# First norm's gain and offset moved behind the gather and into later experts, and a tenth weight tile, in a transformer block with 32 experts

## The chip, the core and the metric

The kernel runs on one core of a Trainium2 chip. A core has TensorE (PE, matrix multiplies, with its weight loads shown apart as PEld), VectorE (DVE), ScalarE (ACT), GpSimd (POOL) and the issuing engine SyncE (SP). Sixteen transfer engines (DMA) move data between the chip's memory (HBM), the on-chip SBUF and the accumulators of TensorE (PSUM). The metric is the time of one execution on the device, in microseconds (us).

## The reference

One layer of an encoder over 256 tokens of 1024 numbers, in float32. The first half is attention in two branches with gates; it ends in an output projection. What the change touches is what follows:

```python
x = layer_norm(ALPHA * x + mix, ln1_g, ln1_b)         # mix: the attention half
x = layer_norm(ALPHA * x + moe(x), ln2_g, ln2_b)

def layer_norm(x, g, b):
    return (x - mean(x)) * rsqrt(var(x) + 1e-5) * g + b     # g, b: one number a column

def moe(x):                                            # 32 experts, each token goes to 4
    logits = x @ w_router + b_router                   # 1024 x 32
    top_v, top_i = top_k(logits, 4)
    gates = softmax(top_v)
    # for each token and each of its four experts e:
    h = x @ w_mlp1[e] + b_mlp1[e]                      # 1024 x 2048
    glu, lin = min(h[::2], 7), clip(h[1::2], -7, 7)
    a = glu * sigmoid(1.702 * glu) * (lin + 1)
    y += gate * (a @ w_mlp2[e] + b_mlp2[e])            # 1024 x 1024
```

An expert has 12 MB of weights, all 32 together 403 MB of the 439 MB that the kernel reads.

## The kernel before

**Weights in tiles.** Weights come in tiles of 2 MB (128 partitions of 16 KB), two chunks each. An expert has four tiles for its first layer (`m1`, chunks 0 to 7) and two for its second (`m2`, chunks 0 to 3). `seq` sets the order: `m1` of expert 0, then for each further expert e its `m1` and after it `m2` of expert e - 1, at last `m2` of expert 31. `queue` lists the tiles; `feed` (L88) takes the next and issues its load on SP, `refill` (L120) calls it after a tile's second chunk, into the place just used. SP issues in order: a load waits there until its place is free. Nine places hold weights when the experts begin: five of `ring`, two of `ring2` (freed by the split weights of the first half), `ring4` and `ring3` (in the place `qq`). Other buffers are tags of the pool `big`: "nh", "xh", "xl", "v" and "an" are used one after the other by tiles of different stages.

**From the projection to the experts.** From L588 on the order is written by hand (`manual_schedule`): every engine carries out its part in program order. `residual` forms ALPHA * x + mix and its statistics, `normal` the normed tokens, `affine` (L613) times gain plus offset, three of four halves on GpSimd. `turn` transposes the normed tokens, `logits` multiplies by the router's weights (gain and offset are folded into those, L499) with experts on the partitions, `logits_rows` transposes back. `choose` finds the four experts of each token, `count` and `place` its slot in each expert (64 slots, CAP), `pick` builds a matrix P of ones that says which token sits in which slot, and `gather_mm` (L704) multiplies the tokens by P: `XS`, the transposed tokens of four experts, in eight column blocks k.

**In the experts.** `m1` multiplies `XS` by the weights into two PSUM banks, copies the result to `hs`; `activate` transposes it, adds the bias and applies the gate; `m2` multiplies by the second layer's weights into one bank ("tp"), `gate_o` scales it by the gate and splits it in two float32r parts `oh` and `ol`; `combine` (L835) adds them, by token, to Y in PSUM. `onehot` prepares the combine's matrix. What else is done beside is hung by `at` behind a chunk: the gather of the next four experts (L892 to L894), the biases of the second layers at expert 8, the loading and spreading of the second norm's gain and offset (`load_ln2` behind chunk 1 of expert 28's first layer, `spread_ln2` (L874) behind chunks 3 and 4 of experts 29's and 30's first layers). Y starts as ALPHA times the first norm's result: `y_start` (L844), four multiplies by a scaled unit matrix `alid`, three in the router stretch and one behind chunk 1 of expert 1.

**The end.** After the last combine the statistics of Y are completed, and the second norm is applied and stored.

The functions, with the profile's line numbers:

Of the kernel before, what the change touches and what calls it, by code (L numbers as in the profile page):

```python
# [17 lines left out]
D = 1024  # L18
NE = 32
# [12 lines left out]
def block_kernel(ctx: ExitStack, tc: tile.TileContext, x, xT, w_in, cols_in, b_v, lam_v,  # L32
# [55 lines left out]
    def feed(where=ring_tile):  # L88
# [22 lines left out]
        kind, e, c = seq[2 * u - N1]  # L111
# [48 lines left out]
    br = keep.tile([NE, 2], F32, name="br")  # L160
# [385 lines left out]
    for i in range(N1):  # L546
# [11 lines left out]
        if i == N1 - 1:  # L558
            for j in range(SPL):
# [9 lines left out]
        if i == 23:  # L569
            feed(lambda: big.tile([128, 4096], F32, name="ring3", tag="qq"))  # L570
# [19 lines left out]
    x1 = big.tile([128, 2, D], F32, name="x1", tag="nh")  # L590
# [37 lines left out]
    def logits(t):  # L628
        pl = pp.tile([128, 512], F32, name="tp", bufs=1)
# [3 lines left out]
        lt_ = keep.tile([NE, 128], F32, name="lgT", bufs=1)  # L633
        act(lt_, pl[:NE, 0:128], AF.Identity, bias=br[:, 1:2])
        lgs[t] = lt_

    def logits_rows(t):
        p = pp.tile([128, 512], F32, name="pv", bufs=1)
        nc.tensor.transpose(p[:, 0:NE], lgs[t], ident[:NE, :NE])
        lgs[t] = p  # L640

    def choose(t):
        pl = lgs[t][:, 0:NE]
        m8 = keep.tile([128, 8], F32, name="m8", bufs=2)
        nc.vector.max(out=m8, in_=pl)
        nm = keep.tile([128, 2], F32, name="nm", bufs=2)
# [486 lines left out]
```

## Time and profile before

| | us |
|---|---|
| median of 3 runs (lowest, highest) | 1158.22 (1156.41, 1159.78) |
| the profiled execution | 1158.14 |
| its span, first to last instruction | 1156.4 |
| TensorE busy in the span | 1060.6 (92%) |
| VectorE, ScalarE, GpSimd busy | 368.7, 221.6, 29.1 |
| transfers: 440.83 MB, mean | 381 GB/s |

The page gives busy time by engine, strips of 40 slices, the chain of work that ended last, and the costliest groups of instructions. A busy TensorE is one with a multiply under way, which includes slow ones. "DMA share" is the mean busy share of the 16 transfer engines and can pass 1 a little, since packets overlap. In the timeline a row merges neighbouring instructions of one form; in square brackets stands how long the engine had been idle before it, and what released it. A multiply in float32 is carried out in two passes and counts as two instructions.

### The profile page before, as it was taken

How to read it: one execution, taken by the hardware profiler on the slowest of the kernel's cores; microseconds unless marked ns; L12 is line 12 of the kernel's file. 1: busy time of each engine (PE TensorE's matmuls, PEld its weight loads, DVE VectorE, ACT ScalarE, POOL GpSimd, SP SyncE). 2: the span in 40 equal slices, each digit the busy share in tenths (PEclk: the TensorE clock that was granted, in tenths of full speed). 3: DMA queues.
4: the chain of work that ended last, by engine and by line, in shares of the span. 5: the costliest groups of instructions: out<-in, count | busy, mean ns of one | idle time of the engine just before them, and what ended most of it. 6: DMA issues, size and time to landing. Idle time of an engine off the chain costs nothing.

```text
span 1156.4 us, 12728 instructions
## 1 busy us (share of the span) xinstructions
PE 1060.6 (92%) x5318; PEld 500.7 (43%) x5318; DVE 368.7 (32%) x772; ACT 221.6 (19%) x423; POOL 29.1 (3%) x34
## 2 busy tenths in 40 slices
PE   9999999899999999899899989888999899989984
PEld 8888898533433433333333333332333333322221
DVE  6967757332222222222222122222222221222213
ACT  5475843221111111010001000100010000001111
POOL 0001100200000000000000000000000000000001
PEclk9999999999999999999999999999999999999997
DMA  9953468599999999999999999999999999999992
GB/s 339 382 173 110 164 255 333 216 392 425 426 427 426 426 404 426 426 428 429 426 427 426 427 427 428 427 426 427 426 429 425 427 426 426 427 427 427 427 423 110
DMA packets 48318, 440.83 MB, mean 381 GB/s; under 512 B 5376, under 2 KB 8576, under 8 KB 23424
## 3 DMA queue, kind: packets, MB, share of 16 engines
q1 hardware_dynamic: 47696, 438.91, 91.5%
q8 instruction: 44, 0.72, 0.3%
q0 software_dynamic: 272, 0.53, 0.1%
q10 hardware_dynamic: 288, 0.52, 0.1%
q14 instruction: 18, 0.15, 0.0%
HBM read 438.90 MB, written 1.05 MB: 380 GB/s over the span
## 4 chain that ended last, share of the span: by engine, by line
DMA 57%; PE 29%; issue 6%; DVE 4%; ACT 3%; SPq 0%; POOLq 0%; POOL 0%; ACTq 0%
DMA ring<-in_w_dram 55%; PE sc L773 12%; PE tp L818 5%; PE pj L256 3%; PE pj L440 2%; DMA ring<-in_w_in_dram 2%; PE tp L708 1%; PE pv L708 1%; DVE sp L46 1%; PE pj L271 1%; DMA b1r<-in_b_dram 1%; DVE tm L46 1%; ACT sp L43 1%; PE sc L792 1%; PE pj L841 1%
## 5 line engine op out<-in xcount | busy, mean ns | idle before, releaser
L773 PE MATMUL sc<-ring,XS 128*64 128x512 f32 x2048 | 473.0, 599 | 49.4 <-DMA ring<-in_w_dram 48.7
L773 PEld LDWEIGHTS sc<-ring,XS 128*64 128x64 f32 x2048 | 138.4, 136 | 327.5 <-issue 268.3
L818 PE MATMUL tp<-ring,work 128*64 128x512 f32 x1024 | 235.3, 599 | 20.3 <-DMA ring<-in_w_dram 18.6
L818 PEld LDWEIGHTS tp<-ring,work 128*64 128x64 f32 x1024 | 68.5, 136 | 160.8 <-issue 115.9
L781 DVE COPY hs<-sc 128x512 f32<-128x512 f32 x32 | 22.1, 692 | 320.8 <-PE sc L773 320.8
L256 PE MATMUL pj<-XH,sp 128*128 128x256 f32 x512 | 96.6, 288 | 3.9 <-DVE sp L46 3.6
L256 PEld LDWEIGHTS pj<-XH,sp 128*128 128x128 f32 x512 | 80.6, 192 | 8.3 <-DVE sp L46 4.7
L737 DVE TENSOR_SCALAR GT<-pv,slotp 128x256 fp32r<-128x256 f32 x32 | 15.5, 484 | 197.9 <-PE pv L735 197.9
L46 DVE TENSOR_TENSOR sp<-ring,sp 128x1024 fp32r<-128x1024 f32 (+1 forms) x58 | 68.1, 1188 | 27.2 <-ACT sp L43 27.0
L256 PE MATMUL pj<-XL,sp 128*128 128x256 f32 x256 | 73.2, 286 | 0.0
L43 ACT ACTIVATE sp<-ring 128x1024 fp32r<-128x1024 f32 (+1 forms) x58 | 58.0, 1023 | 67.1 <-PE pj L256 31.0
L46 DVE TENSOR_TENSOR work<-sc,bT 128x512 f32<-128x512 f32 x62 | 42.6, 688 | 74.1 <-PE sc L792 74.1
L43 ACT ACTIVATE as<-work 128x256 f32<-128x256 f32 x64 | 26.7, 417 | 165.0 <-DVE work L799 165.0
L831 DVE SCALAR_TENSOR_TENSOR ol<-tp,GS,oh 128x512 fp32r<-128x512 f32 x32 | 24.0, 751 | 93.8 <-ACT oh L43 93.8
L43 ACT ACTIVATE XS<-pv 128x256 f32<-128x256 f32 x32 | 12.3, 383 | 210.1 <-PE pv L708 210.1
L256 PEld LDWEIGHTS pj<-XL,sp 128*128 128x128 f32 x256 | 49.2, 192 | 0.6 <-issue 0.6
L43 ACT ACTIVATE XS<-tp 128x256 f32<-128x256 f32 x32 | 12.3, 383 | 193.1 <-PE tp L708 193.1
L43 ACT ACTIVATE oh<-tp,GS 128x512 fp32r<-128x512 f32 x32 | 22.0, 687 | 111.4 <-PE tp L818 111.4
L792 PEld LDWEIGHTS sc<-ident,hs 128*128 128x128 f32 x248 | 32.1, 209 | 25.1 <-issue 25.1
L43 ACT ACTIVATE hs<-sc 128x512 f32<-128x512 f32 x32 | 19.1, 597 | 112.9 <-PE sc L773 109.1
L792 PE MATMUL sc<-ident,hs 128*128 128x128 f32 x248 | 38.0, 296 | 0.0
L708 PE MATMUL pv<-P,x 128*128 128x256 f32 x128 | 35.5, 401 | 0.0
(200 smaller groups left out, 742.3 us busy)
## 6 DMA issues: line engine op xcount, KB each, us to landing
ring<-in_w_dram SPq DMA_DIRECT2D x190, 2048.0 KB, 39.1
ring<-in_w_in_dram SPq DMA_DIRECT2D x17, 1024.0 KB, 13.6
ring<-in_w_out_dram SPq DMA_DIRECT2D x4, 1024.0 KB, 6.7
ring<-in_w_dram SPq DMA_DIRECT2D x4, 1024.0 KB, 33.1
ring<-in_w_in_dram SPq DMA_DIRECT2D x4, 512.0 KB, 7.8
nb<-in_rpbx_dram SPq DMA_DIRECT2D x8, 256.0 KB, 3.8
ring<-in_w_da_dram SPq DMA_DIRECT2D x2, 1024.0 KB, 6.1
ring<-in_w_na_dram SPq DMA_DIRECT2D x2, 1024.0 KB, 8.4
```

The source lines that it names most:

```text
L43: return nc.scalar.activation(o, i, f, **kw)
L46: return nc.vector.tensor_tensor(out=o, in0=a, in1=b, op=op)
L256: nc.tensor.matmul(pj[g][:, c], lhsT=a(k, cc), rhs=b[:, kk], start=(kk == 0 and j == 0 and c % 2 == 0), stop=(kk == 7 and j == 2), skip_gr ...
L271: nc.tensor.matmul(pj[g][:, h], lhsT=a[:, kk, hh], rhs=b(k), start=(kk == 0 and j == 0), stop=(kk == 7 and j == 2), skip_group_check=True)
L440: nc.tensor.matmul(y[:, c], lhsT=a(k, cc), rhs=b[:, k], start=(k == 0 and j == 0 and c % 2 == 0), stop=(k == 3 and j == 2), skip_group_che ...
L708: nc.tensor.matmul(px, lhsT=v, rhs=P[g][:, t], start=(t == 0), stop=(t == 1))
L737: nc.vector.tensor_scalar(GT[e], p[:, 256:512], slotp[:, 0:1], None, op0=ALU.is_equal)
L773: nc.tensor.matmul(HP[h][j * CAP:(j + 1) * CAP], lhsT=XS[e // 4][:, c, e % 4], rhs=w[:, h, j], start=(c == 0), stop=(c == 7), skip_group_c ...
L781: nc.vector.tensor_copy(HS[e][:, 1], HP[1])
L792: nc.tensor.transpose(p[:, s, k], v[:, s, k], ident)
L818: nc.tensor.matmul(OP[e][j * CAP:(j + 1) * CAP], lhsT=AS[e][:, c, k], rhs=ring[i][:, n:n + 512], start=(c + k == 0), stop=(c == 3 and k == ...
L831: nc.vector.scalar_tensor_tensor(out=ol, in0=OP[e], scalar=GS[e], in1=oh.bitcast(F32), op0=ALU.mult, op1=ALU.subtract)
```

## The change

1. The first norm's gain and offset are no longer applied to all tokens. `gather` gathers the normed tokens of two experts (columns of 128 instead of 256 a multiply), for two column blocks a call, and ScalarE applies gain and offset as scale and bias of the copy to `XS` (`gbx`, loaded by two GpSimd loads).
2. `residual` and `normal` work in place; the tile `x1` ("nh") goes. `XS` is one tile of two halves in "xh", so "xl" is free too. `hs` and `work` share one tile.
3. "nh" and "xl" hold the two halves of a tenth weight tile (`ring5`), loaded as 1 MB each by `feed_half`: the first behind chunk 23 of the first half, the second behind its last.
4. Y starts with the first combine. ALPHA times the first norm's result is added in experts 3 to 6, a quarter each: `x1_load` fetches gain and offset of both halves into the tile of `oh` (GpSimd, behind chunk 1), `x1_part` spreads one row over the partitions by a multiply and VectorE multiplies or adds it (behind chunks 3 and 4), `y_x1` adds the quarter to Y (behind chunk 6).
5. `logits` has the tokens on the partitions at once, with the bias as a ninth multiply of one row; the ScalarE bias and `logits_rows` go. Copies that only the gates need are taken later (`keep_logits`). The first layers' biases are loaded to "v" and transposed in two halves.
6. The second norm's gain and offset and the output use the first place that is not `ring` and that falls free when no weights are left; they are spread behind the chunks of expert 30's second layer.

```diff
+    def feed_half(s):
+        if s == 0:
+            half[0] = queue.pop(0) if queue else None
...
+        t = ring[2 * u + s] = big.tile([128, 2048], F32, name="ring5", tag=("nh", "xl")[s])
+        if kind == "m1":
+            nc.sync.dma_start(t, m1c(e, c // 2)[:, s])
+        else:
+            nc.sync.dma_start(t.rearrange("p (k c) -> p k c", k=2), m2c(e, c // 2)[:, 2 * s:2 * s + 2])
     def refill(i):
-        if i % 2:
-            feed(home[i // 2])
+        where = home[i // 2]
+        if where == "half":
+            feed_half(i % 2)
+        elif i % 2:
+            if not queue and where is not ring_tile and not lnt:
+                load_ln2(where())
+            else:
+                feed(where)
...
-    def affine(t, h, eng=nc.vector):
-        v = x1[:, t, cut(h)]
-        eng.tensor_tensor(out=v, in0=xn[:, t, cut(h)], in1=late["g"][:, cut(h)], op=ALU.mult)
-        eng.tensor_tensor(out=v, in0=v, in1=late["b"][:, cut(h)], op=ALU.add)
...
+        pl = lgs[t] = pp.tile([128, 512], F32, name=("tp", "pv")[t], bufs=1)
         for k in range(8):
-            nc.tensor.matmul(pl[:NE, 0:128], lhsT=wr[:, k], rhs=x1T[:, k, t * 128:(t + 1) * 128],
-                             start=(k == 0), stop=(k == 7))
+            nc.tensor.matmul(pl[:, 0:NE], lhsT=x1T[:, k, t * 128:(t + 1) * 128], rhs=wr[:, k], start=(k == 0), stop=False)
+        nc.tensor.matmul(pl[:, 0:NE], lhsT=ones[0:1], rhs=br[:, 1], start=False, stop=True)
...
+    def gather(g, k0):
+        px = pp.tile([128, 2, 2, CAP], F32, name="pv" if k0 % 4 else "tp", bufs=1)
+        for u in range(2):
+            k = k0 + u
+            for t in range(2):
+                v = xn[:, t].rearrange("q (c p r) -> q c r p", p=128, r=2)[:, k // 2, k % 2]
+                nc.tensor.matmul(px[:, u], lhsT=v, rhs=P[g][:, t], start=(t == 0), stop=(t == 1))
+        for u in range(2):
+            k = k0 + u
+            act(XS[g][:, k], px[:, u], AF.Identity, scale=gbx[:, 0, k:k + 1], bias=gbx[:, 1, k:k + 1])
...
+    def x1_load():
+        gb = p2b.tile([4, 512], F32, name="gb", tag="oh", bufs=1)
+        for j, src in enumerate((ln1_g, ln1_b)):
+            nc.gpsimd.dma_start(gb[2 * j:2 * j + 2], src.rearrange("(h n) -> h n", h=2))
+        x1p[:] = [gb, p2b.tile([128, 512], F32, name="x1p", tag="ol", bufs=1)]
+    def x1_part(t, h, j):
+        p = pp.tile([128, 512], F32, name="pv", bufs=1)
+        gb, v = x1p
+        nc.tensor.matmul(p, lhsT=ident[0:4, 2 * j + h:2 * j + h + 1].to_broadcast([4, 128]), rhs=gb, start=True, stop=True)
+        tt(v, v if j else xn[:, t, cut(h)], p, ALU.add if j else ALU.mult)
+    def y_x1(t, h):
+        nc.tensor.matmul(Y[t][:, h], lhsT=lstrict, rhs=x1p[1], start=False, stop=False, skip_group_check=True)
...
+            for k in ((0, 2), (4, 6))[e % 2] if e > 1 else ((0,), (2, 4, 6))[e]:
+                at(("m1", e, 5 if e else 7), gather, g, k)
...
+    for e in range(4):
+        t, h = divmod(e, 2)
+        at(("m1", e + 3, 1), x1_load)
+        at(("m1", e + 3, 3), x1_part, t, h, 0)
+        at(("m1", e + 3, 4), x1_part, t, h, 1)
+        at(("m1", e + 3, 6), y_x1, t, h)
...
-    at(("m1", NE - 4, 1), load_ln2)
     for j in range(2):
         for h in range(2):
-            at(("m1", NE - 3 + j, 3 + h), spread_ln2, j, h)
+            at(("m2", NE - 2, 2 * j + h), spread_ln2, j, h)
...
     turn(0)
+    logits(0)
     normal(1)
-    logits(0)
-    affine(1, 0)
-    affine(1, 1, nc.gpsimd)
-    y_start(0, 1)
+    choose(0)
     turn(1)
-    logits_rows(0)
-    choose(0)
-    y_start(0, 0)
     logits(1)
...
+    gather(0, 0)
+    bias_turn(1)
     m1(N1, *seq[0][1:])
-    for k in range(3, 5):
-        gather_mm(0, k)
+    gather(0, 2)
     m1(N1 + 1, *seq[1][1:])
```

How the instructions stand on TensorE from the second logits to the first expert multiplies, before (`x_2037` is the tokens' tile after `affine`, `ring_1577` the first weight tile, L773 `m1`, L846 `y_start`, L756 the transposes of the first layers' biases):

```order
L631 MATMUL tp<-x1T,wr 32x128 x8
L664 MATMUL sc<-maskM,lstrict 128x32
L639 MATMUL pv<-ident,lgT 128x32
L756 MATMUL tp<-ident,b1r 128x64 x8
L663 MATMUL sc<-maskM,ones 128x32
L664 MATMUL sc<-maskM,lstrict 128x32
L846 MATMUL pj<-x_2037,alid 128x512
L708 MATMUL tp<-P,x_2037 128x256 x2
L708 MATMUL pv<-P,x_2037 128x256 x2
L708 MATMUL tp<-P,x_2037 128x256 x2
L773 MATMUL sc<-ring_1577,XS 64x512 x4
```

and now (`xres` is the tokens' tile, L651 and L652 `logits`, L781 the biases, L731 `gather`, L796 `m1`):

```order
L651 MATMUL pv<-wr,x1T 128x32 x8
L652 MATMUL pv<-br,ones 128x32
L680 MATMUL sc<-maskM,lstrict 128x32
L679 MATMUL sc<-maskM,ones 128x32
L680 MATMUL sc<-maskM,lstrict 128x32
L781 MATMUL sc<-ident,b1r 128x64 x4
L731 MATMUL tp<-P,xres 128x128 x4
L781 MATMUL sc<-ident,b1r 128x64 x4
L796 MATMUL sc<-ring_1578,XS 64x512 x4
```

The transposes of the logits and three multiplies into Y are gone, the bias transposes stand in two halves, the second behind the first gather, and one gather of four multiplies stands ahead of the first expert multiplies where three gathers stood.

TensorE in expert 3's first layer, before (L841 `combine`, L735 `onehot`, L708 the gather, L818 `m2`):

```order
L773 MATMUL sc<-ring_2375,XS 64x512 x8
L841 MATMUL pj<-oh,GT 128x512 x4
L841 MATMUL pj<-ol,GT 128x512 x4
L773 MATMUL sc<-ring_2412,XS 64x512 x4
L735 MATMUL pv<-rows,stack 128x512
L773 MATMUL sc<-ring_2412,XS 64x512 x4
L773 MATMUL sc<-ring_2422,XS 64x512 x8
L708 MATMUL tp<-P,x_2037 128x256 x2
L708 MATMUL pv<-P,x_2037 128x256 x2
L773 MATMUL sc<-ring,XS 64x512 x8
L818 MATMUL tp<-ring,work 64x512 x4
```

and now (L864 is `combine`, its second half stands in the first row, L760 `onehot`, L880 `x1_part`, L885 `y_x1`):

```order
L864 MATMUL pj<-ol,GT 128x512 x4
L796 MATMUL sc<-ring,XS 64x512 x4
L760 MATMUL pv<-rows,stack 128x512
L796 MATMUL sc<-ring,XS 64x512 x4
L880 MATMUL pv<-gb,ident 128x512
L796 MATMUL sc<-ring_2415,XS 64x512 x4
L880 MATMUL pv<-gb,ident 128x512
L796 MATMUL sc<-ring_2415,XS 64x512 x4
L731 MATMUL tp<-P,xres 128x128 x4
L731 MATMUL pv<-P,xres 128x128 x4
L796 MATMUL sc<-ring_2425,XS 64x512 x4
L885 MATMUL pj<-x1p,lstrict 128x512
```

Two multiplies by `gb` and one into Y have come in between the chunks; the gather's two calls stay where they were.

TensorE at the end, from the second layer of expert 30 on, before (L818 `m2`, L792 the transposes of expert 31's activation, L841 `combine`):

```order
L818 MATMUL tp<-ring_5746,work 64x512 x4
L792 MATMUL sc<-ident,hs 128x128 x8
L818 MATMUL tp<-ring_5746,work 64x512 x4
L818 MATMUL tp<-ring_5762,work 64x512 x8
L818 MATMUL tp<-ring,work 64x512 x8
L841 MATMUL pj<-oh,GT 128x512 x4
L841 MATMUL pj<-ol,GT 128x512 x4
L818 MATMUL tp<-ring,work 64x512 x8
```

and now (L841 is `m2`, L815 the transposes, L915 `spread_ln2`, L864 `combine`; `ring_6172` is the tile of gain and offset):

```order
L841 MATMUL tp<-ring_6041,hsas 64x512 x4
L815 MATMUL sc<-ident,hsas 128x128 x8
L915 MATMUL pv<-ring_6172,ones 128x512
L841 MATMUL tp<-ring_6041,hsas 64x512 x4
L915 MATMUL pv<-ring_6172,ones 128x512
L841 MATMUL tp<-ring_6066,hsas 64x512 x4
L915 MATMUL pv<-ring_6172,ones 128x512
L841 MATMUL tp<-ring_6066,hsas 64x512 x4
L915 MATMUL pv<-ring_6172,ones 128x512
L841 MATMUL tp<-ring_6076,hsas 64x512 x8
L864 MATMUL pj<-oh,GT 128x512 x4
L864 MATMUL pj<-ol,GT 128x512 x4
```

The four spreads stand now between and behind the chunks of expert 30's second layer. ScalarE's row there, before (`as` is the activation's sigmoid, `warm` the preloading of a table, `oh` empties the second layer's bank):

```order
L43 ACTIVATE hs<-sc 128x512
L43 ACTIVATE as<-work 128x256 x2
L43 ACT_TABLE_LOAD
L43 ACTIVATE warm<-as,eps 1x1
L43 ACTIVATE oh<-tp,GS 128x512 x2
```

and now:

```order
L43 ACTIVATE hsas<-sc 128x512
L43 ACTIVATE as<-gl 128x256 x2
L43 ACT_TABLE_LOAD
L43 ACTIVATE warm<-as,eps 1x1
L43 ACTIVATE ring_6172<-pv 128x512 x3
L43 ACTIVATE oh<-tp,GS 128x512
L43 ACTIVATE ring_6172<-pv 128x512
```

The copies of the spreads stand behind the activation and the table load, three of them ahead of the emptying of expert 30's bank.

## Rows read from the trace of the kernel before

**Rows 1.** The page's strip of GB/s, 40 equal slices of the span

```profile
GB/s 339 382 173 110 164 255 333 216 392 425 426 427 426 426 404 426 426 428 429 426 427 426 427 427 428 427 426 427 426 429 425 427 426 426 427 427 427 427 423 110
```

**Rows 2.** Windows: length, busy time (and count) by engine, granted clock, DMA share, GB/s

```profile
215.00:226.00 11.00, 11.00 (x41) 6.56 (x40) 0.00 (x0) 1.92 (x5) 0.00 (x0) 0.85 0.01 6
236.00:470.00 234.00, 233.66 (x1086) 90.03 (x1084) 57.97 (x141) 27.39 (x57) 2.04 (x4) 1.00 1.01 424
470.00:1121.00 651.00, 583.31 (x2644) 212.36 (x2640) 138.56 (x335) 63.14 (x129) 0.98 (x2) 1.00 1.01 427
```

**Rows 3.** Chain of waits, experts 0 to 6: start us, us, what

```profile
219.44 1.87 PE sc L773 x8
272.33 1.12 PE pj L841 x8
275.75 5.30 PE sc L773 x24
281.05 1.07 PE pv L708 x4
282.12 0.86 PE tp L708 x4
309.69 3.58 PE sc L773 x16
402.40 1.14 PE pj L841 x8
```

**Rows 4.** Timeline of the issue queue SP behind the gap: start us, us, instruction

```profile
225.14 0.33 SPq L118 DMA_DIRECT2D ring<-in_w_dram  x1
232.63 0.33 SPq L113 DMA_DIRECT2D ring<-in_w_dram  x1
```

**Rows 5.** Timeline of the router stretch: start us, us, engine line instruction, idle before

```profile
198.07 1.00 DVE L610 TENSOR_SCALAR xres<-x,bnmv 128x512 f32<-128x512 f32 x2
203.51 1.95 DVE L610 TENSOR_SCALAR xres<-x,bnmv 128x512 f32<-128x512 f32 x2
206.20 1.04 PE L625 MATMUL sc<-ident,xres 128*128 128x128 f32 x8
209.37 1.94 PE L631 MATMUL tp<-x1T,wr 128*32 128x128 f32 x16
212.09 0.20 DVE L645 MAX8 m<-pv 128x8 f32<-128x32 f32 x1 [1.46 <-PE pv L639]
215.14 1.91 PE L708 MATMUL tp<-P,x 128*128 128x256 f32 x4
```

**Rows 6.** DMA issues by tile: queue, count, KB each, us from issue to landing

```profile
wr<-in_w_router_dram SPq DMA_DIRECT2D x1, 128.0 KB, 7.8
work<-in_b_dram POOLq DMA_DIRECT2D x4, 64.0 KB, 7.8
ln<-in_ln_g_dram POOLq DMA_DIRECT2D x1, 4.0 KB, 6.4
ln<-in_ln_b_dram POOLq DMA_DIRECT2D x1, 4.0 KB, 7.2
```

**Rows 7.** Timeline of ln2's spread and of the last two experts

```profile
1051.89 1.12 PE L877 MATMUL pv<-ln,ones 1*128 1x512 f32 x2
1052.94 1.94 PE L773 MATMUL sc<-ring,XS 128*64 128x512 f32 x8
1053.05 0.60 ACT L43 ACTIVATE ln<-pv 128x512 f32<-128x512 f32 x1 [10.78 <-PE pv L877]
1121.36 1.94 PE L818 MATMUL tp<-ring,work 128*64 128x512 f32 x8 [1.34 <-DMA ring<-in_w_dram]
1127.93 0.29 ACT L43 ACTIVATE warm<-as,eps 1x1 f32<-1x1 f32 x1
1131.41 3.65 PE L818 MATMUL tp<-ring,work 128*64 128x512 f32 x16 [1.57 <-DVE ol L831]
```

**Rows 8.** Instructions of line 708: duration ns minimum, median, maximum

```profile
L708 PEld LDWEIGHTS tp<-P,x x128: 192/196/337, 214.6 to 997.5; 128*128 128x128 f32 x128
```

More of the change, by code (lines that the diff above doesn't have):

```diff
@@ L159, in block_kernel @@
     wr = keep.tile([128, 8, NE], F32, name="wr")
-    br = keep.tile([NE, 2], F32, name="br")
+    br = keep.tile([1, 2, NE], F32, name="br")
+    gbx = keep.tile([128, 2, 8], F32, name="gbx")
     make_identity(nc, ident)
@@ L502, in router_fold @@
         for k in range(8):
-            nc.tensor.matmul(p[:NE, 0:1], lhsT=wr[:, k], rhs=b1col[:, k:k + 1], start=(k == 0), stop=(k == 7))
-        tt(br[:, 1:2], br[:, 0:1], p[:NE, 0:1], ALU.add)
+            nc.tensor.matmul(p[0:1, 0:NE], lhsT=b1col[:, k:k + 1], rhs=wr[:, k], start=(k == 0), stop=(k == 7))
+        tt(br[:, 1], br[:, 0], p[0:1, 0:NE], ALU.add)
         tt(wr, wr, g1col.rearrange("p (k o) -> p k o", o=1).to_broadcast([128, 8, NE]), ALU.mult)
@@ L598, in residual @@
     def residual(t, h):
-        v = x1[:, t, cut(h)]
-        nc.vector.scalar_tensor_tensor(out=v, in0=xn[:, t, cut(h)], scalar=ALPHA, in1=OUT[t, h],
-                                       op0=ALU.mult, op1=ALU.add)
+        v = xn[:, t, cut(h)]
+        nc.vector.scalar_tensor_tensor(out=v, in0=v, scalar=ALPHA, in1=OUT[t, h], op0=ALU.mult, op1=ALU.add)
         nc.vector.bn_stats(out=st[t][:, h, :], in_=v)
@@ L835, in combine @@
     def combine(e):
-        for w in OHL[e]:
+        for n, w in enumerate(OHL[e]):
             for t in range(2):
@@ L945, in block_kernel @@
     count(1)
-    y_start(1, 0)
+    bias_turn(0)
     place(1)
     pick(0, slice(1, 2))
-    for k in range(3):
-        gather_mm(0, k)
-    work.append(big.tile([128, 4, 512], F32, name="work", tag="an"))
+    keep_logits(0)
+    keep_logits(1)
+    gather(0, 0)
+    bias_turn(1)
     m1(N1, *seq[0][1:])
-    for k in range(3, 5):
-        gather_mm(0, k)
+    gather(0, 2)
     m1(N1 + 1, *seq[1][1:])
-    for k in range(5, 7):
-        gather_mm(0, k)
+    gather(0, 4)
     m1(N1 + 2, *seq[2][1:])
-    gather_mm(0, 7)
+    gather(0, 6)
     for j, (kind, e, c) in enumerate(seq):
@@ L1047, in block_kernel @@
         row_stats(0)
-    fin = big.tile([128, 2, D], F32, name="fin", tag="qq")
+    lnt, fin = lnt
     row_stats(1)
@@ L1061, in block_kernel @@
         v, y, m = fin[:, t, cut(h)], Y[t][:, h], mv[t]
-        g, b = [lnt[0][:, j, cut(h)] for j in range(2)]
+        g, b = [lnt[:, j, cut(h)] for j in range(2)]
         if (t, h) == (1, 1):
```

141 lines of the change are left out of this document (64 added, 77 removed).

## The prediction

> **What bounds the kernel now.** I read the page's strip of GB/s first [rows 1]: the eighth slice (202 to 231 us) shows 216 between 333 and 392, and from the tenth on nearly all show some 426. The windows say what that is [rows 2]. From 215 to 226 us the transfers stand still (share 0.01), and from 236 to 1121 they never stop (1.01). The nine 2 MB tiles in SBUF are full, and no new one can start before TensorE has used one up: the first issue after the gap stands at 225.14, the second at 232.63 [rows 4], each the refill behind the second chunk of a tile. So nearly all that follows is fixed by when the queue restarts and by how many tiles are then left. The chain of waits bears this out from the other side: it runs through TensorE for the first eight experts, afterwards through the transfers.
>
> TensorE has little to spare at first. From the combine at 272.33 to that at 402.40 lie five experts [rows 3], 26.0 us each. The queue needs 6 x 2.097 MB / 424 GB/s = 29.7 us for the same six tiles [rows 2]. So freed tiles pile up by 3.7 us an expert, and the queue has always one to fill. The third stage is the end: the second multiply of expert 30 starts at 1121.36 behind a transfer, but that of expert 31 waits at 1131.41 for VectorE [rows 7]. From 1121 on TensorE's own order sets the end.
>
> The sum is made against the profiled execution's own 1158.14 us (span 1156.4 and 1.7 around it), 0.08 below the median of the runs.
>
> **The router stretch, earlier restart.** Before, normal(1)'s two halves take 1.95 us at 203.51, beside GpSimd's gains and offsets; normal(0)'s took 1.00 at 198.07, without them. logits(1) starts at 209.37, because TensorE has first to wait for scaled tokens for y_start [rows 5]. Without these, the second half's transposes can start at 204.8 behind logits(0), and logits(1) at 206.1: 3.3 us earlier. It is then 9 multiplies of 32 columns instead of 8 of 128 (1.94 us, row at 209.37). Between the nearest rows I take 2.2. Its end, 208.3, leads straight to VectorE's MAX8; before, a bias on ScalarE and a transpose lay between (209.37 + 1.94 = 211.31 to 212.09). So MAX8 is 3.75 us earlier. The bias transposes, which waited for b1, fall out of this path, since b1 now lands in a tile that is free long before; one half of them is back behind the gather. A y_start in front of the gather goes too, and P's comparison is half as wide: the first gather starts at 210.75 (before 215.14). Before, three gathers led to the expert multiplies of which the row at 219.44 is the first [rows 3]; now one gather and four transposes: 212.5 us at full clock. The granted clock was 0.85 in the mean of 215 to 226 [rows 2], so part of it was at the lower level of 1.2 GHz, after a stretch of short multiplies with gaps. A dip as long would give 214.3. I take 213.4. One gather and two chunks later (5.75 us before, 4.85 now) the first tile is free at 218.2, 6.9 us earlier; the next at 225.2, **7.4 us earlier**.
>
> **The tenth tile.** All ten are loaded before 218, since half one of it fits where the queue idles and half two follows the output projection. When the queue restarts, one tile less is left: 2.097 MB / 427 GB/s = **4.9 us**. Its halves go in 8 KB runs instead of 16 KB. A run's fixed part, an estimate: w_in's runs of 2 KB filled the second slice at 382 GB/s, the 16 KB runs move 427 [rows 1, 2], which per transfer engine (a sixteenth) is 86 and 614 ns a run, so 12 ns a run beside its bytes. Twice the runs in 18 tiles cost 18 x 4.9 x 12/614 = **1.8 us**, between nothing and twice that. If the queue then never starves, the gain is 7.4 + 4.9 - 1.8 = 10.5 us.
>
> **What experts 3 to 6 add.** Each gets three f32 multiplies of 512 columns (two by the broadcast gain and offset, one into Y). Such a one, spread_ln2's, let the next multiply begin 1.05 us later (1051.89 to 1052.94, its busy time 1.12) [rows 7], and a switch of weights costs the next chunk 0.1 to 0.15 (1.87 against 5.30/3) [rows 3]: 3.6 us in all. Of the four y_start removed one stood in expert 1: 1.3 us with its switch. The gather of 128 columns costs more per column: 8 transposes of 128 x 128 took 1.04 us, 0.13 each [rows 5], so a call of 8 parts 1.05 for 0.86 before, and two calls an expert 2.3 for 1.93 [rows 3]: 0.4 more.
>
> And there is a new wait. x1_load's two GpSimd loads overwrite the tile that combine's first half reads. I put their issues at 0.85 and 1.35 us after combine starts: two thirds of its 1.12, and half a us for each issue. TensorE reaches x1_part 5.2 us after that start (combine 1.12, chunk 1.87, the one-hot up to 275.75, a chunk of 5.30/3) [rows 3]. The nearest rows are the two 4 KB loads of the last norm, 6.4 and 7.2 us from issue to landing in a busy queue [rows 6]: the second lands 7.75 to 8.55 after the start. TensorE stands 2.55 to 3.35; I take 2.7, as a queue that has just run dry is less deep. Behind x1_part stand all expert multiplies and thus the next release.
>
> So an expert takes 26.0 + 0.4 + 3.6 + 2.7 = 32.7 us against 29.7: 3.0 us short. What is in hand? From the second release to the last of expert 3's first layer, TensorE took 309.69 + 3.58 - 232.63 = 80.6 us [rows 3, 4]; now 80.6 - 1.3 + 0.2 + 1.4 - 0.5 + 0.4 (y_start; gathers of experts 0 to 3: 1, 3, 2, 2 calls for 1, 2, 3, 2 before) + 3.6 + 2.7 = 87.1. In that time the queue fills 18 tiles, 89.0 us. In hand: 1.9. Experts 4 to 6 lose 3 x 3.0 - 1.9 = **7.1 us**. Of the 10.5, 3.4 remain.
>
> The Trainium skill (DMA: Bandwidth & Descriptors, "Anatomy of one DMA") puts a GpSimd load at about 2.0 us and its bytes. By that gain and offset would be there before TensorE asks, and nothing of the 7.1 us would be lost. The loads of 6.4 and 7.2 us speak against it here; it is a rival below.
>
> **The tail.** spread_ln2 moves from experts 29 and 30, where TensorE waits for transfers, to behind the four chunks of expert 30's second layer. One spread takes 1.05 as above, its copy 0.60 [rows 7]. The first, behind the transposes, ends at 1125.5, but its copy stands on ScalarE behind the activations and the table preload, until 1128.2 [rows 7]. They share one PSUM bank, so the second spread, ready at 1127.3, waits till 1128.85. Third and fourth chunk end at 1131.7 and 1134.6, the third spread between. ScalarE and VectorE empty the bank as before (1.57 us, which hides the fourth): expert 31 starts at 1136.1 instead of 1131.41: **4.7 us later**. Lower bound 0, if the transfers end last after all; upper, 4 x 1.6.
>
> **Small things.** The two gbx loads are 1024 runs of 8 bytes at the start, when the queue is full; wr is as many runs of 128 bytes and landed in 7.8 us beside others [rows 6]. Between nothing and 1.5 us, I take 0.5. The additional ScalarE copies of XS are hidden: TensorE needs them an expert later, and ScalarE is free between.
>
> **Sum:** -10.5 + 7.1 + 4.7 + 0.5 = +1.8: **1159.9 us**.
>
> **Rivals.** *The gain stays* (1152.8): no stall, so 30.0 an expert against 29.7, covered by what is in hand; -10.5 + 5.2. It needs the second load within 3.9 us of its issue; every load on that queue in rows 6 took longer, but none was so small beside an almost empty queue. Half of the stall gone gives 1154.5.
> *Late loads* (1164.9; the slower side): the loads behave like the four of b2, 7.8 us [rows 6], and TensorE stands 3.95 us. 1.25 more an expert in three experts, and nearly as much in the first, is 5 us. Each us of stall costs 4 us, so it is slower than can be told from no change once the second load takes over 7.0 us. For it: the rows of b2 and of the norm's second load, 7.2, lie there. Against: only two rows of 2 KB travel. *Weights exposed* belongs to the same side: a 128 x 128 weight load of the gather took 0.196 us [rows 8]; if no part of it were hidden, a call would take 1.57, 1.0 us more an expert and 4 us up to expert 3: 1166.9. The Trainium skill (TensorE: Matmul & The Clock Gate, "LDWEIGHTS") says that the load costs by its own columns, however few are moved; halving the moved columns doubles the loads per result. The 0.13 us of the transposes says that most is hidden.
> *The tail's spreads cost nothing* (1155.2): the last transfers would have to end later than TensorE's order; the wait on VectorE at 1131.41 is against it.
>
> **Chances.** The measurement tells about 0.3% (3.5 us) from no change. Forecast, within some 4 us of its sum: 0.40. The gain stays: 0.28. Late loads or exposed weights: 0.27. Free tail: 0.05, which stays within 3.5 us of before. The upper end of the forecast's own range, 0.03, is beyond 3.5 us. Faster 0.28, same 0.42, slower 0.30. The likeliest case alone spans 1155 to 1163; with the rivals until two in ten are left, 1151 to 1166.
>
> **What would show it.** Right: an issue after the gap near 218 and no more than 5 us of standing transfers there; in experts 3 to 6, x1_part's multiply released by the load of gb after 2 to 3.5 us, and the DMA share below 1 at 340 to 420 us; the second spread idle before ScalarE's copy, and expert 31's second layer 4 to 5 us later behind expert 30's. Wrong: x1_part without a wait, a share that stays at 1.01 from 236 on, or an end chain that runs through transfers to the last us.

## The result and the profile after

The changed kernel takes 1173.05 us in the median (lowest 1170.98) where the kernel before takes 1157.32 in the same rounds: ratio 1.0128, 95% interval 1.0100 to 1.0157. One of its four executions took 1555.64 us at a granted clock of 0.648; the ratio leaves it out, the median does not. The forecast was 1159.9 with a range up to 1166. The profiled execution took 1170.98 (span 1169.2, 12.8 more than before).

The strips of the page, granted clock and GB/s in 40 slices of 29.2 us, already say where:

```profile
PEclk9999999899889999999999999999999999999997
GB/s 337 378 169 113 167 227 369 313 427 426 408 383 354 339 371 411 428 426 427 428 426 428 426 428 425 427 429 427 428 426 425 430 428 426 427 427 429 427 407 51
```

Before, the rate stayed at some 426 from the tenth slice on [rows 1]. Now it sinks from the eleventh to the sixteenth (292 to 468 us), and two of these slices show a lower clock. The three windows of [rows 2], and below them the stretch of experts 3 to 6 in four parts (busy time by engine, granted clock, DMA share, GB/s):

```profile
215.00:226.00 11.00, 10.10 (x58) 4.93 (x56) 0.00 (x0) 4.12 (x10) 0.00 (x0) 1.00 0.56 203
236.00:470.00 234.00, 223.64 (x995) 83.85 (x989) 56.09 (x134) 28.36 (x61) 6.10 (x12) 0.94 0.95 390
470.00:1121.00 651.00, 606.09 (x2949) 236.12 (x2949) 145.68 (x356) 84.63 (x181) 0.98 (x2) 1.00 1.01 427
...
300.00:330.00 30.00, 29.39 (x122) 10.89 (x124) 6.62 (x14) 3.73 (x8) 0.98 (x2) 0.89 0.98 398
330.00:360.00 30.00, 27.27 (x103) 10.04 (x101) 7.08 (x17) 3.04 (x7) 0.01 (x1) 0.83 0.83 330
360.00:390.00 30.00, 27.42 (x111) 9.19 (x109) 3.76 (x8) 2.89 (x6) 1.00 (x2) 0.89 0.87 355
390.00:420.00 30.00, 27.84 (x124) 10.18 (x121) 7.18 (x17) 3.13 (x7) 0.98 (x2) 0.94 0.97 385
```

The transfers stand for some 4.8 of the first window's 11 us, where they stood for nearly all of it before (share 0.56 for 0.01); the third stage runs at the same 427 GB/s. Between them the granted clock is 0.83 to 0.94: 30 us times (0.11 + 0.17 + 0.11 + 0.06) are 13.5 us of TensorE's time. No term of the prediction holds them.

TensorE in expert 4, from the one-hot to the second multiply by `gb`, in the timeline (L760 `onehot`, L796 `m1`, L880 `x1_part`):

```profile
330.98 0.49 PE L760 MATMUL pv<-rows,stack 96*128 96x512 f32 x1
331.40 1.94 PE L796 MATMUL sc<-ring,XS 128*64 128x512 f32 x8
336.07 1.09 PE L880 MATMUL pv<-gb,ident 4*128 4x512 f32 x2 [2.73 <-DMA gb<-in_ln_b_dram]
337.09 3.10 PE L796 MATMUL sc<-ring,XS 128*64 128x512 f32 x8
340.12 2.07 PE L880 MATMUL pv<-gb,ident 4*128 4x512 f32 x2
```

and windows of 3 us over it:

```profile
335.00:338.00 3.00, 1.93 (x6) 0.63 (x8) 0.80 (x2) 0.00 (x0) 0.00 (x0) 0.95 0.96 410
338.00:341.00 3.00, 3.00 (x7) 0.74 (x4) 0.22 (x1) 0.00 (x0) 0.00 (x0) 0.50 1.02 437
...
344.00:347.00 3.00, 3.00 (x12) 1.39 (x9) 0.00 (x0) 0.00 (x0) 0.00 (x0) 0.50 0.88 330
...
350.00:353.00 3.00, 3.00 (x12) 0.78 (x10) 0.00 (x0) 0.09 (x1) 0.00 (x0) 1.00 0.08 33
```

The wait is 2.73 us; the forecast put it at 2.7. Less than 2 us after it has ended the clock falls to 0.50, that is 1.2 GHz, for about 10 us, and the same chunk or multiply takes up to twice as long (1.09 at 336.07, 2.07 at 340.12). A little later the transfers have nothing left to fill (share 0.08). The waits of the other three experts are 2.55, 2.58 and 2.16 us; each is followed by such a fall, of 3 to 7 us.

The issues behind the gap and the end of the kernel, against [rows 4, 7] (L841 `m2`, L915 the spread, `ring` in ScalarE's row its copy):

```profile
219.32 0.33 SPq L113 DMA_DIRECT2D ring<-in_w_dram  x1
...
226.51 7.74 SPq L113 DMA_DIRECT2D ring<-in_w_dram  x3
...
1129.58 1.94 PE L841 MATMUL tp<-ring,hsas 128*64 128x512 f32 x8 [1.12 <-DMA ring<-in_w_dram]
...
1134.85 1.28 ACT L43 ACT_TABLE_LOAD   x1
...
1136.35 0.57 ACT L43 ACTIVATE ring<-pv 128x512 f32<-128x512 f32 x1
...
1136.97 1.12 PE L915 MATMUL pv<-ring,ones 1*128 1x512 f32 x2 [1.37 <-ACT ring L43]
...
1144.45 3.65 PE L841 MATMUL tp<-ring,hsas 128*64 128x512 f32 x16 [0.52 <-DVE ol L854]
```

The second issue comes 6.1 us earlier (226.51 for 232.63). The second layer of expert 30 starts 8.2 us later (1129.58 for 1121.36), and expert 31's 14.87 us behind it instead of 10.05, which is 4.8 more. From these rows comes the account used below. What the queue lost in between is the shift of 1129.58, less the shift of the second issue, plus the 4.9 us of the tenth tile: 8.2 + 6.1 + 4.9 = **19.2 us**, where the forecast had 7.1 (and 1.8 for the halves' runs). A rate that differs by 0.2% would move this by 2 us; e10 below, with nine tiles as before, needs 886.7 us for the way from the second issue to expert 30's second layer where the kernel before needs 888.7, so the account is good to some 2 us.

### The profile page after: what moved, and what is told of

It is laid out like the page before. It is cut to its first block, busy times and chain, and to the rows that moved or that the text cites. A ratio compares the mean times of both kernels' runs of the same rounds, so it can differ in the third digit from the quotient of the medians.

```text
span 1169.2 us, 13431 instructions
## 1 busy us (share of the span) xinstructions
PE 1085.4 (93%) x5592; PEld 522.1 (45%) x5592; DVE 369.6 (32%) x786; ACT 247.9 (21%) x487; POOL 25.2 (2%) x38
## 3 DMA queue, kind: packets, MB, share of 16 engines
HBM read 437.89 MB, written 1.05 MB: 375 GB/s over the span
## 4 chain that ended last, share of the span: by engine, by line
DMA 44%; PE 21%; issue 3%; POOL 0%; POOLq 0%; SPq 0%
DMA ring<-in_w_dram 42%; PE sc L796 10%; PE tp L841 6%; PE sc L815 1%; DMA gb<-in_ln_b_dram 1%; PE tp L731 1%; PE pj L864 1%; PE pv L731 1%; DMA ring<-in_ln_g_dram 0%; PE pv L880 0%; PE pv L760 0%; PE pj L903 0%; PE pj L885 0%; POOLq L1162 0%; POOL ring L1098 0%
## 5 line engine op out<-in xcount | busy, mean ns | idle before, releaser
L796 PE MATMUL sc<-ring,XS 128*64 128x512 f32 x2048 | 482.1, 608 | 33.5 <-DMA ring<-in_w_dram 33.0
L796 PEld LDWEIGHTS sc<-ring,XS 128*64 128x64 f32 x2048 | 138.4, 138 | 307.3 <-issue 254.9
L841 PE MATMUL tp<-ring,hsas 128*64 128x512 f32 x1024 | 234.9, 598 | 14.5 <-DMA ring<-in_w_dram 14.0
L841 PEld LDWEIGHTS tp<-ring,hsas 128*64 128x64 f32 x1024 | 69.1, 136 | 153.6 <-issue 122.5
L804 DVE COPY hsas<-sc 128x512 f32<-128x512 f32 x32 | 22.1, 692 | 310.5 <-PE sc L796 310.5
L43 ACT ACTIVATE XS<-tp,gbx 128x128 f32<-128x128 f32 x64 | 25.8, 453 | 416.7 <-PE tp L731 414.8
L46 DVE TENSOR_TENSOR gl<-sc,bT 128x512 f32<-128x512 f32 x62 | 42.6, 687 | 66.0 <-PE sc L815 66.0
L43 ACT ACTIVATE as<-gl 128x256 f32<-128x256 f32 x64 | 26.7, 416 | 153.7 <-DVE gl L822 153.7
L731 PEld LDWEIGHTS tp<-P,xres 128*128 128x128 f32 x256 | 34.1, 204 | 26.1 <-issue 25.9
L815 PEld LDWEIGHTS sc<-ident,hsas 128*128 128x128 f32 x248 | 32.4, 210 | 25.2 <-issue 25.2
L731 PE MATMUL tp<-P,xres 128*128 128x128 f32 x256 | 40.3, 303 | 0.1
L815 PE MATMUL sc<-ident,hsas 128*128 128x128 f32 x248 | 38.2, 297 | 0.0
```

Of the source, the lines that this page charges most:

```text
L43: return nc.scalar.activation(o, i, f, **kw)
L46: return nc.vector.tensor_tensor(out=o, in0=a, in1=b, op=op)
L731: nc.tensor.matmul(px[:, u], lhsT=v, rhs=P[g][:, t], start=(t == 0), stop=(t == 1))
L796: nc.tensor.matmul(HP[h][j * CAP:(j + 1) * CAP], lhsT=XS[e // 2][:, c, e % 2], rhs=w[:, h, j], start=(c == 0), stop=(c == 7), skip_group_c ...
L804: nc.vector.tensor_copy(HS[e][:, 1], HP[1])
L815: nc.tensor.transpose(p[:, s, k], v[:, s, k], ident)
```

## The experiments

Theory: the waits for `gb` make the granted clock fall after them, and it is this fall, more than the wait or the added multiplies, that starves the queue. Rivals: the multiplies with 4 rows lower the clock; the wait costs its own length only; the added work is the loss. In the table "clock" is the time lost to a granted clock under 1 from 300 to 420 us, "queue" the account above; all from the profiled execution of each.

| kernel | median us | ratio to before, 95% | waits for gb, us | clock, us | queue, us |
|---|---|---|---|---|---|
| the change | 1173.05 | 1.0128 (1.0100 to 1.0157) | 10.0 | 13.5 | 19.2 |
| e1, gb loaded early | 1154.57 | 0.9977 (0.9966 to 0.9989) | 0 | 0 | -0.4 |
| e2, before with waits | 1158.04 | 1.0005 (0.9995 to 1.0016) | 9.7 | 3.6 | |
| e3, waits filled | 1160.83 | 1.0045 (1.0024 to 1.0066) | 1.0 | 0 | 6.8 |
| e4, no spreads | 1169.73 | 1.0109 (1.0066 to 1.0152) | 9.8 | 17.7 | 23.5 |
| e8, 128 rows | 1170.50 | 1.0123 (1.0100 to 1.0145) | 12.9 | 8.7 | 16.1 |
| e11, wait apart | 1166.28 | 1.0070 (1.0043 to 1.0098) | 9.7 | 5.4 | 11.0 |
| e12, a chunk later | 1153.25 | 0.9957 (0.9944 to 0.9969) | 3.6 | 0 | -0.2 |

**e1, the wait taken away.**

```diff
-        gb = p2b.tile([4, 512], F32, name="gb", tag="oh", bufs=1)
...
+        if not x1p:
+            gb = p2.tile([8, 256], F32, name="gb")
...
+    at(("m1", 1, 5), x1_load)
```

Gain and offset are loaded once, behind chunk 5 of expert 1's first layer, and each multiply by `gb` becomes two of 256 columns.

> The first norm's gain and offset are loaded once, in expert 1, into a small tile of their own; the multiplies of experts 3 to 6 stay (as two of 256 columns each, with 8 rows). Theory (the wait of 2.2 to 2.7 us makes the granted clock fall to 0.5 afterwards): no idle time ahead of these multiplies and a granted clock of 1.00 from 296 to 420 us; the 18.4 us that the queue loses between 300 and 470 us shrink to 1 or less, and the time to about 1155.5 us. Rival (it is the multiplies with only 4 or 8 rows that lower the clock): the 10 us of idle time go, the 13.6 us lost to the lower clock stay, TensorE needs some 33.4 us an expert for the queue's 29.7, and the time is about 1164.

Measured 1154.57. The clock is 1.00 from 300 to 420 us, with multiplies of 8 rows in the same places; this is the window of expert 4:

```profile
330.00:360.00 30.00, 30.00 (x145) 11.76 (x139) 7.87 (x19) 3.73 (x8) 0.00 (x0) 1.00 1.01 427
```

So the multiplies do not lower the clock by themselves, and the added work alone costs the queue nothing. As the queue account is about zero here, the 8 KB runs of the tile's halves cost nothing that stands out of its 2 us either.

**e3, the wait filled with work.**

```diff
+        if j == 0:
+            for n in 512, 512, 256:
+                nc.tensor.matmul(p[:, 0:n], lhsT=ident, rhs=xn[:, t, 0:n], start=True, stop=True)
```

> The changed kernel, with three multiplies in float32 (512, 512 and 256 columns, their result overwritten) ahead of the first multiply by gb in each of experts 3 to 6, so that TensorE is at work while the loads of gb travel. Theory: no idle time of more than 0.5 us there, a granted clock of 1.00 in 296 to 420 us; TensorE still loses the length of the wait, as the prediction had it (32.7 us an expert, 7.1 us lost by the queue instead of 18.4): about 1162. Rival (the multiplies of 4 rows lower the clock, or the added work itself is the loss): clock and time stay, 1173.

Measured 1160.83. Expert 4's wait is gone into multiplies, the rate sinks only a little, and the clock stays. This is the row of its first multiply by `gb`, with no wait before it:

```profile
333.36 1.09 PE L883 MATMUL pv<-gb,ident 4*128 4x512 f32 x2
```

And this is the window of expert 4:

```profile
330.00:360.00 30.00, 29.89 (x136) 11.43 (x134) 6.98 (x17) 3.73 (x8) 1.00 (x2) 1.00 0.99 404
```

TensorE still loses the length of the wait, yet the kernel is 12 us faster than the change. The queue loses 6.8 us, where the prediction had worked out 7.1 for just this case: wait and work, no fall. Its multiplies by `gb` stand 32.1 to 32.4 us apart, where the prediction had 32.7. The profiled execution (1158.96) is the fastest of eight; three others took 1164.5 to 1166.5 at a mean granted clock of 0.984 to 0.987 instead of 0.992, so in those the clock was low for longer, at a place that no profile shows.

**e2, the wait alone in the kernel before.**

```diff
+    for e in range(3, 7):
+        at(("m1", e, 1), lone_load)
+        at(("m1", e, 3), lone_wait)
```

`lone_load` loads gain and offset into the tile of `oh`, `lone_wait` is one multiply of 4 rows and 8 columns by them.

> The kernel before, with only the loads of gain and offset into the tile of oh in experts 3 to 6 and one multiply of 4 rows and 8 columns behind them that waits for them; nothing is added to Y by it. Theory (wait, then low clock): four waits of 2 to 3 us, each followed by 3 to 10 us at a granted clock of 0.5; 26.0 + 2.7 + 3.4 = 32.1 us an expert against 29.7, with 8.4 us in hand at expert 3, lose some 5 us: about 1162.5. Rival (the wait costs its own length only): 28.7 us an expert are less than 29.7, the clock stays at 1.00, and the time is 1157.3 as before.

Measured 1158.04, no difference that can be told: the theory's 1162.5 was too much. The waits are there, but the clock fell behind two of the four only (at 335.19 and 393.44):

```profile
306.91 0.19 PE L917 MATMUL pv<-gb,ident 4*4 4x8 f32 x2 [2.56 <-DMA gb<-in_ln_b_dram]
335.19 0.19 PE L917 MATMUL pv<-gb,ident 4*4 4x8 f32 x2 [2.09 <-DMA gb<-in_ln_b_dram]
364.63 0.19 PE L917 MATMUL pv<-gb,ident 4*4 4x8 f32 x2 [2.43 <-DMA gb<-in_ln_b_dram]
393.44 0.19 PE L917 MATMUL pv<-gb,ident 4*4 4x8 f32 x2 [2.61 <-DMA gb<-in_ln_b_dram]
```

So a fall behind such a wait is no certainty, and without the work of `x1_part` TensorE's lead (3.7 us an expert) covers wait and fall: these rows stand 28.3 to 29.4 us apart, under the queue's 29.7.

**e8 and e11, what stands behind the wait.** e8 gives the multiplies 128 rows, all but four of them zero; e11 leaves a tiny multiply in their place and puts them behind chunks 6 and 7, and the one into Y behind the second layer's chunk 1. e8's edit:

```diff
-        gb = p2b.tile([4, 512], F32, name="gb", tag="oh", bufs=1)
+        gb = p2b.tile([128, 512], F32, name="gb", tag="oh", bufs=1)
+        nc.vector.memset(gb, 0.0)
...
```

and e11's:

```diff
-        at(("m1", e + 3, 3), x1_part, t, h, 0)
-        at(("m1", e + 3, 4), x1_part, t, h, 1)
-        at(("m1", e + 3, 6), y_x1, t, h)
+        at(("m1", e + 3, 3), lone_wait)
+        at(("m1", e + 3, 6), x1_part, t, h, 0)
+        at(("m1", e + 3, 7), x1_part, t, h, 1)
+        at(("m2", e + 2, 1), y_x1, t, h)
```

> The changed kernel, with gain and offset in a tile of 128 rows, the others zero (one memset by VectorE ahead of the loads), so that the multiplies by gb have 128 rows instead of 4; the wait ahead of them stays or grows by some 0.5 us. Theory A (any wait of over 2 us, whatever follows): dips of the granted clock as in the changed kernel (13.6 us lost in 300 to 420 us), time about 1173 to 1176. Theory B (the wait together with the multiplies of 4 rows that follow; in e2, where full chunks follow, only two waits of four were followed by a dip, of some 1.7 us loss each): dips as in e2, some 3.5 us lost in place of 13.6, time about 1163 to 1165.

> The changed kernel, with the wait for gb in experts 3 to 6 at a multiply of 4 rows and 8 columns in its old place (behind chunk 3), and the two multiplies by gb behind chunks 6 and 7 instead, the one into Y behind the first chunk of the second layer. Theory B (the wait and the multiplies by gb right behind it together): the clock falls as little as in e2 (some 3.5 us lost in 300 to 420 us), the time is about 1163. Theory A (the wait alone, with what is behind it of no account): 8 to 18 us lost to the clock as in the changed kernel, about 1170.

Measured 1170.5 and 1166.28, both between their theories. In e8 the clock fell behind all four waits (2.81 to 3.49 us), in e11 behind three; the one without a fall was this:

```profile
405.29 0.19 PE L885 MATMUL pv<-gb,ident 4*4 4x8 f32 x2 [1.49 <-DMA gb<-in_ln_b_dram]
```

The few rows are thus not needed for a fall. Why the falls last 3 us in e2 and e11, up to 10 in the change and 14 in e4 stays open.

**e12, the wait made shorter.**

```diff
-        at(("m1", e + 3, 3), x1_part, t, h, 0)
-        at(("m1", e + 3, 4), x1_part, t, h, 1)
-        at(("m1", e + 3, 6), y_x1, t, h)
+        at(("m1", e + 3, 4), x1_part, t, h, 0)
+        at(("m1", e + 3, 6), x1_part, t, h, 1)
+        at(("m1", e + 3, 7), y_x1, t, h)
```

> The changed kernel, with the two multiplies by gb behind chunks 4 and 6 and the one into Y behind chunk 7, a chunk later than in the changed kernel: the loads are issued as before, so the wait is a chunk (1.87 us) shorter, 0.3 to 0.9 us instead of 2.2 to 2.7. Theory (the clock falls behind waits of over 2 us only): granted clock 1.00 from 296 to 420 us, 31 us an expert at most, some 2 us lost by the queue, time about 1157. Rival (any wait there, or the order of the multiplies, lowers the clock): time falls by the shorter wait alone, some 7 us: 1166.

Measured 1153.25, 20 us less than the change, by multiplies that come a chunk later. The waits that are left, in the timeline:

```profile
301.26 1.09 PE L880 MATMUL pv<-gb,ident 4*128 4x512 f32 x2 [1.17 <-DMA gb<-in_ln_b_dram]
331.79 1.09 PE L880 MATMUL pv<-gb,ident 4*128 4x512 f32 x2 [0.87 <-DMA gb<-in_ln_b_dram]
362.37 1.09 PE L880 MATMUL pv<-gb,ident 4*128 4x512 f32 x2 [0.93 <-DMA gb<-in_ln_b_dram]
392.70 1.09 PE L880 MATMUL pv<-gb,ident 4*128 4x512 f32 x2 [0.68 <-DMA gb<-in_ln_b_dram]
```

and the window of expert 4:

```profile
330.00:360.00 30.00, 29.13 (x137) 10.77 (x135) 7.53 (x17) 3.73 (x8) 1.00 (x2) 1.00 1.01 426
```

Work and loads are those of the change, a chunk later; with waits of 0.68 to 1.17 us the clock stays at 1.00 in this stretch and the queue loses nothing.

The profiled execution is the slowest of e12's eight (1157.86), and its end shows why: behind the second spread, which waits for ScalarE's copy as in the change, the clock is at 0.50 from 1119.5 to 1133.5.

```profile
1110.47 1.94 PE L841 MATMUL tp<-ring,hsas 128*64 128x512 f32 x8 [1.16 <-DMA ring<-in_w_dram]
...
1117.86 1.12 PE L915 MATMUL pv<-ring,ones 1*128 1x512 f32 x2 [1.38 <-ACT ring L43]
...
1121.82 2.07 PE L915 MATMUL pv<-ring,ones 1*128 1x512 f32 x2
...
1129.43 5.57 PE L841 MATMUL tp<-ring,hsas 128*64 128x512 f32 x16
```

Expert 31's second layer starts 18.96 us behind expert 30's instead of 14.87. The same wait of 1.37 or 1.38 us stands in seven profiles; in e5, e11 and e12 a fall follows, in the change, e1, e3 and e8 none. The three with a fall are executions 4.5 to 5.7 us above their kernel's median.

**e4 and e6, the tail.** The second norm's gain and offset are loaded to all partitions by SP; no spreads. e4 is the change with it, e6 is e1 with it.

```diff
-            nc.gpsimd.dma_start(lnt[0][0:1, j], bc(src, 1))
+            nc.sync.dma_start(lnt[0][:, j], bc(src))
...
-            at(("m2", NE - 2, 2 * j + h), spread_ln2, j, h)
```

> The changed kernel, with the second norm's gain and offset loaded by SP to all 128 partitions (1 MB) and no spreading by TensorE and ScalarE. Theory (the spreads cost the tail 4.8 us): the second layer of expert 31 starts 10 us behind that of expert 30 instead of 14.9, and the time is 4.8 us less, about 1168.2. Rival (the 1 MB stands in the way of the last weights, or the last norm waits for it): 2.5 us of the gain go, about 1170.7, or no gain.

> The kernel of e1_early_gb, with the second norm's gain and offset loaded by SP to all 128 partitions and not spread by TensorE. Theory (the spreads cost the tail 4.8 us, and that is most of what e1 still loses): 4.8 us under e1, about 1149.8; the second layer of expert 31 starts 10 us behind that of expert 30. Rival (the 1 MB collides with the last weights): 1152 or more.

The second layers of experts 30 and 31 in e4:

```profile
1135.55 1.94 PE L841 MATMUL tp<-ring,hsas 128*64 128x512 f32 x8 [1.33 <-DMA ring<-in_w_dram]
...
1145.58 3.65 PE L841 MATMUL tp<-ring,hsas 128*64 128x512 f32 x16 [1.57 <-DVE ol L854]
```

10.03 us apart, 4.84 less than in the change, and the end follows as before. e4's times scatter from 1166.1 to 1175.8, so its median (1169.73) can't show the term; e6 can: 1149.28, ratio 0.9928 (0.9910 to 0.9945), 5.3 under e1. No cost of the 1 MB shows.

**e5, e7, e9, e10: the router stretch, the tile, the best version.** e5 is e1 with the logits' multiplies 128 columns wide. e7 is the change with `x1_load`, `x1_part` and `y_x1` in experts 15 to 18, e5's logits and e6's loads; e9 is e7 with narrow logits, e10 is e7 without the tenth tile.

```diff
-            nc.tensor.matmul(pl[:, 0:NE], ..., rhs=wr[:, k], ...)
+            nc.tensor.matmul(pl[:, 0:128].rearrange("p (a e) -> p a e", a=4), ...,
+                             rhs=wr[:, k:k + 1].to_broadcast([128, 4, NE]), ...)
...
-        at(("m1", e + 3, 1), x1_load)
+        at(("m1", e + 15, 1), x1_load)
```

> The kernel of e1_early_gb, with the logits' multiplies 128 columns wide (the router's 32 columns four times over; only the first 32 results are read). Theory (the multiplies that move only 32 columns let the granted clock fall in the router stretch, to 0.50 from 205 to 219 us in e1's profile and from 208 to 214.6 in that of the changed kernel): the clock stays at 1.00 from 200 to 225, the second issue behind the gap stands at about 223 instead of 229.7, and the time is 4 to 6 us under e1's 1154.6: about 1149. Rival (it is the waits of TensorE for other engines that lower it): the clock falls as before, and the time is e1's or, by longer multiplies, 1 us above.

> The changed kernel with the residual added in experts 15 to 18 instead of 3 to 6 (loads and waits as in the changed kernel), with the wide logits of e5 and the loads of e6. Theory: in experts 15 to 18 TensorE waits for transfers anyway, and ten full tiles cover a slower expert; the waits and the low clock stand in the trace, but the transfers do not stop. Restart 9.4 us earlier than the kernel before and one tile less (4.9 us), end as before: about 1143. Rival (the waits cost transfers there too, some 8 us an expert less what the tiles cover): up to 10 us more, 1153.

> The kernel of e7_best with the logits' multiplies 32 columns wide again. Theory (the width of these multiplies decides whether the granted clock falls in the router stretch): a stretch at 0.50 between 205 and 219 us, 6 to 14 us long, the second issue behind the gap at 226.5 to 229.7 instead of 225.35, and a time 1 to 4.5 us above e7's 1145.1: about 1148. Rival (the clock falls there by other causes, and e7's profile without a fall is chance): 1145 as e7, and stretches at 0.50 in both.

> The kernel of e7_best without the tenth tile (neither of its halves is loaded; nine places). Theory (a tile less behind the gap is worth its transfer, and the 8 KB runs of its halves cost nothing measurable, since e1's queue moves 427 GB/s as before's): 4.9 us above e7, about 1150.0. Rival of the prediction (the halves' runs cost 1.8 us): 3.1 us above, about 1148.2.

Medians: e5 1151.06, ratio 0.9942 (0.9925 to 0.9960); e7 **1145.13**, 0.9894 (0.9877 to 0.9910), the fastest of all (its theory had 1143); e9 1148.56, 0.9915 (0.9887 to 0.9942); e10 1150.05, 0.9930 (0.9904 to 0.9956). e10 lies 1150.05 - 1145.13 = 4.9 us above e7, but the intervals overlap, and in its profile the second issue stands at 226.68, 1.3 us behind e7's 225.35. So it does not tell the theory's 4.9 us for the tenth tile from its rival's 3.1. The wide logits give 3.5 (e1 to e5, whose intervals stand apart) and 3.4 (e9 to e7, whose intervals overlap). The router stretch in e7, in two windows:

```profile
205.00:210.00 5.00, 4.54 (x35) 3.87 (x33) 1.74 (x13) 1.09 (x2) 0.00 (x0) 1.00 1.03 437
210.00:215.00 5.00, 4.58 (x26) 2.83 (x26) 1.38 (x9) 1.58 (x6) 0.55 (x1) 1.00 1.02 436
```

and the same two in e9:

```profile
205.00:210.00 5.00, 4.75 (x26) 4.45 (x24) 0.68 (x6) 1.08 (x2) 0.00 (x0) 0.63 1.02 388
210.00:215.00 5.00, 4.85 (x23) 4.21 (x23) 2.02 (x14) 0.75 (x3) 0.55 (x1) 0.50 1.00 423
```

The wide form takes hardly longer than the narrow one at full clock (16 passes in 2.05 us for 1.97). It does not exclude a fall: in e5's profile 212 to 216 us were at 0.50 all the same, so the theory's "1.00 from 200 to 225" is not met there, and its second issue stands at 226.21 where the theory had 223 (e1: 229.7). But the low clock of this stretch lasts 6.6 to 13.7 us in all nine profiles with 32 columns, and nothing to 3.5 us in the three with 128 (e5, e7, e10). In experts 15 to 18 of e7 the four waits stand (10.8 us in all) and each is followed by a fall, but the transfers run on (share 1.00 or 1.01 from 630 to 750 us):

```profile
660.00:690.00 30.00, 27.16 (x102) 9.29 (x100) 6.21 (x14) 3.48 (x8) 0.00 (x0) 0.83 1.00 425
```

## Why the prediction was wrong

- **Earlier restart**, 7.4 us forecast: 6.1 measured. The order of the terms held (second MAX8 at 208.85 instead of 208.3), but the low clock of the router stretch lasted 6.6 us (208.0 to 214.6) where the kernel before shows some 3.
- **The tenth tile**, 4.9: not shown by itself. e7 restarts 7.3 us earlier than the kernel before, and 7.3 + 4.9 = 12.2 us against 11.8 measured speaks for it; e10 doesn't tell it from 3.1.
- **Runs of 8 KB**, 1.8: open. The accounts of e1 and e12 come to -0.4 and -0.2 us with them, and the third stage moves 427 GB/s as before, but the account is good to some 2 us only. The two rates of the estimate give 10 ns a run beside its bytes instead of 12, which makes 1.5 us.
- **Work and wait of experts 3 to 6**: the parts were right. A gather call takes 1.04 us (309.50 to 310.54; 1.05 forecast), which also ends the rival of exposed weight loads; a multiply by `gb` 1.02 at full clock (336.07 to 337.09); the waits 2.16 to 2.73 (2.7). The loads landed 5.2 to 6.4 us after their issue, so the rival of late loads did not come about, though the time fell on its side. The Trainium skill's 2.0 us for a GpSimd load (DMA: Bandwidth & Descriptors, "Anatomy of one DMA") is a third of that here.
- **The step that failed** is "So an expert takes 26.0 + 0.4 + 3.6 + 2.7 = 32.7 us": it counts the wait by its length and all else at full clock. The rows of `gb` stand 35.5, 37.1 and 35.1 us apart, 3.2 more in the mean, which over four experts comes near the 13.5 us of low clock. With it, 7.1 + 13.5 = 20.6 us against 19.2 measured; without it (e3) 6.8 against 7.1. The prediction had seen such a fall in [rows 2] (0.85 from 215 to 226) and priced it in the router stretch alone. What spoke against it elsewhere were the waits of the third stage in the kernel before, none of which is over 1.8 us or followed by a fall:

```profile
PE sc L773 <- DMA ring<-in_w_dram: 48.7, 49, 1.8
```

Even such a wait is not safe: in e12's profile one of 1.83 us was followed by 0.50 for 3.4 us.

```profile
948.67 3.39 PE L796 MATMUL sc<-ring,XS 128*64 128x512 f32 x8 [1.83 <-DMA ring<-in_w_dram]
```

- **The tail**, 4.7: 4.8 measured, in the way forecast (the second spread waits for the copy behind the table load). That is the profile without a fall behind this wait; with one the tail costs some 4 us more (e12), and the prediction did not price it here either.
- **Small loads at the start**, 0.5: the first `normal` stands at 198.29 for 198.07, 0.2.

Together: -6.1 - 4.9 + 19.2 + 4.8 = 13.0 us; the span grew by 12.8. As the 19.2 was itself worked out from where expert 30's second layer starts, this sum checks the end alone; what supports the 19.2 is 7.1 + 13.5, and e3.

## What to carry to other kernels

A new wait on the engine that releases the transfers is priced with what its clock does afterwards, not by its length: here 10 us of waits brought 13.5 us of low clock with them. Where the engine has little lead, put the consumer one unit of work later, load its data earlier or fill the wait; in these runs the first and the second brought the time under that of the kernel before. A short wait is no safeguard by itself: one of 1.38 us at the end was followed by a fall in three profiles of seven. Where it waits for transfers anyway, the same wait and fall cost the transfers nothing (e7). The tail, where one engine's order sets the end, is no place for work that a transfer can do.

## What the runs showed of the hardware

Of 32 waits for `gb` of 1.49 to 3.49 us in eight profiles (the change, e2, e4, e7 to e11), 28 were followed by a granted clock of 0.50 for 3 to 14 us; the four without were 1.49, 2.43, 2.47 and 2.56 us long, so length alone does not decide. None of the four of 0.68 to 1.17 us in e12 was, but three of seven waits of 1.37 or 1.38 us at the end were. Times scatter differently too: e4, with the falls in the way, over 9.7 us, e7, where they are covered, over 1.2; e3, whose profile shows none in experts 3 to 6, still over 7.5. In the router stretch the clock fell for 6.6 us in the change and for 13.7 in e1, whose program is the same up to there.
